# Layer 0's MLP in eight groups of 512 features, with seven block products from the third group on

## The chip, the cores and the metric

The kernel runs on one core of a Trainium2 chip. Its time is the time of one execution on the device in microseconds (us); three runs of the kernel before give 1492.6, 1496.15 and 1498.59 us, median 1496.15. One more execution was recorded by the profiler; all rows below are from that one.

A core has a matrix engine (PE; its weight loads are listed as PEld), a vector engine (DVE), a scalar engine (ACT), a general engine (POOL), and SP, which here only issues DMAs. Each works through its own instructions in a fixed order, and semaphores make one wait for another.

## The reference, cut to what matters

The program is a two-layer encoder trunk over 528 positions (512 frames and 16 meta tokens) of 1024 channels. Layer 0 has retention and an RG-LRU, layer 1 an S5 state space model and HGRN2; every layer ends with an MLP between two RMS norms:

```python
def rms_norm(x, g):
    return x * rsqrt(mean(x * x, axis=-1) + EPS) * g

# in each layer, D_FF = 4096
f = rms_norm(h, pre_g) @ w1            # 528x1024 @ 1024x4096
f = square(relu(f)) @ w2               # 528x4096 @ 4096x1024
h = h + rms_norm(f, post_g)
```

S5 needs factors that depend on its parameters only (powers of a complex number per state, their products with B and C, cosine and sine tables); layer 0's time is used to prepare them.

## The kernel before, in words

**Numbers.** All matrices are fp32. A factor is split into a rounded part (`wh`, `ah`, `nh`) and the rest (`wl`, `al`, `nl`), and a product is three matmuls: high by high, high by low, low by high (`three`, line 540). ACT writes the rounded part (CAST or ACTIVATE), DVE subtracts it to get the rest. Every weight matrix that is used thus costs ACT one cast and DVE (or POOL) one subtraction per element, besides its DMA.

**Layout.** Channels lie on the 128 partitions, positions along the free axis, in two halves of 264. A matmul takes 128x128 weights and 264 positions. `pair` gives a PSUM pair for both halves.

**Weights.** `weights` (line 410) writes down the order of all weight chunks of the program in a list, `plan`. `fetch` (439) issues a chunk's DMA to a `raw` buffer, `prepare` (460) splits all chunks up to a number, and `chunk` (474) hands out the next one after fetching two ahead and splitting one ahead. A chunk has 128x8x256 elements (1 MB).

**Order.** Each engine's order is that in which the Python program emits instructions. Work beside the matmuls is written as generators; `spawn` (373) puts one on a list, and `tick` (392), which the matrix loops call every few matmuls, lets those run whose time by a running estimate has come. A number that a generator yields is its wish for a pause. `drain` (403) runs all that is left.

**Layer 0's MLP** (`mlp0`, 1500) goes in four quarters of 1024 features. In a quarter, `mlp_in` (1374) multiplies by four chunks of the first matrix (tiles `m` on PE), and the result is squared after relu: ACT relu, ACT `ah`, ACT square into `mr`, DVE `mr`, DVE `al`. Then come four chunks of the second matrix, whose products DVE adds to eight accumulators `y` in SBUF. The last two chunks of the last quarter go through `gemm_trail` (722), which does all of the first half of the positions, then the second, so that the norm and the residual (`Stream.residual`, 897) of one half run beside the matmuls of the other. The next layer starts with `gemm_lead` (695), which takes the two halves likewise, with tiles `lead` on PE.

**Layer 1's MLP** does the first matrix of its last three quarters by seven block products instead of eight (Strassen's way in Winograd's form): channels and positions are each cut into halves, class `Seven` (630) makes sums and differences of weight blocks on POOL (`ws`, and in place in `raw`), splits them, and `seven_evac` (1452) joins the products `p` in PSUM into four results by seven additions on DVE (`mr`). The sums of the moving side are made once, before, by `moving_sums` (1407).

**S5's preparation** (`s5_prepare`, 1665) runs beside layer 0's MLP. `s5_common` (1558) makes the powers; `s5_half` (1611), eight times, the factors of four groups each: six POOL instructions of 128x512 in two runs of `powers` (`w`, `pt`, `m2`), transposes on PE, and small matmuls `k0`; `s5_tables` (1644), four times, the cosine and sine tables `ct`, `st` with scratch `tm`, by complex products (`cmul`, 362) on POOL. Tiles print as `m` for `m1`, `m2`, and `k` for `k0`.

Of the kernel before, what the change touches and what calls it, by code (L numbers as in the profile page):

```python
# [73 lines left out]
def trunk(ctx, tc, io, out, dbg=None):  # L74
# [436 lines left out]
    for l in range(2):  # L511
# [13 lines left out]
        for q in range(4):  # L525
            for i in range(4):
                seven = l == 1 and q > 0
                weights(w1s[l], 0, q * D + CW * i, order="S" if seven else "")
            if l == 0:
                for cc in range(4):  # L530
                    weights(w2s[l], q * D, CW * cc)
                continue
# [83 lines left out]

    def split_halves(i):
# [12 lines left out]
    class Seven:  # L630
# [7 lines left out]
        def __init__(self, n0, pairs):  # L638
            self.n0, self.pairs, self.n = n0, pairs, 14 * pairs
            self.fed, self.ops, self.s = 0, {}, {}  # L640

        def feed(self, upto):

            while self.fed < min(upto, self.n):
# [21 lines left out]
                (G if prod in ("P3", "P4") else V).tensor_tensor(lo, src, hi.bitcast(F32), SUB)  # L666
# [8 lines left out]
        def run(self, xops, evac):  # L675

            last = (self.n + 3) // 4 - 2
            for i in range(self.n):
                self.feed(i + 8 - i % 4 if i % 4 == 0 else i + 8)
# [7 lines left out]
                for k in range(4):  # L687
                    three(ps[:, e, :256], (hi, lo), k, 0, ops[k], k == 0, k == 3)
                    if k % 2:
                        tick()  # L690
                if e:
                    evac(pair_, prod, ps[:, :, :256])
# [173 lines left out]
    class Stream:  # L866
# [3 lines left out]
        def __init__(self, l, n, cut, keep=None, packed=True, lag=20.0):  # L870
            self.l, self.n, self.cut, self.keep, self.packed, self.lag = l, n, cut, keep, packed, lag
            self.ready, self.summed = [False, False], [False, False]
            self.sums = Squares(cut)
# [500 lines left out]
    def mlp_in(l, q, st):  # L1374
# [13 lines left out]

        if q == 0:
            gemm_lead([(w1s[l], 0, CW * i) for i in range(2)], st, cut, st.ready, evac)  # L1390
        elif l == 1:
            until(lambda: len(moving[4]) == 4)
            seven[0].run(lambda prod: moving_of(st, prod), seven_evac(a2))
            return a2
        for i in range(2 if q == 0 else 0, 4):
            wc = chunk(w1s[l], 0, q * D + CW * i)
# [8 lines left out]
    seven, moving = [None], {n: [] for n in (1, 2, 3, 4)}  # L1405

    def moving_sums(st):
# [3 lines left out]
        fst, snd = slice(0, 256), slice(256, 512)  # L1411
        for c in range(4):
            if c % 2 == 0:
                units = [(U("th", F32R), U("tl", F32R)) for _ in range(4)]
            cs = slice((c % 2) * 256, (c % 2) * 256 + 256)
# [17 lines left out]
            yield 3.0  # L1433

    def moving_of(st, prod):
        n = {"P5": 1, "P6": 2, "P7": 3, "P4": 4}.get(prod)
        if n:
            return moving[n]
# [3 lines left out]
    class Halves:  # L1442
# [5 lines left out]
        def __getitem__(self, at_):  # L1448
            c0, c1 = at_[1].start, at_[1].stop
            return self.parts[c0 // 256][:, c0 % 256 : c0 % 256 + c1 - c0]  # L1450

    def seven_evac(a2):
# [3 lines left out]
        def both(t):  # L1456
            return t[:, :512].rearrange("p (e w) -> p e w", e=2)

        def square(j, h, r):
            hi, lo = U("ah", F32R)[:, :512], U("al", F32R)[:, :512]  # L1460
# [6 lines left out]
        def evac(pair_, prod, ps):  # L1467
            def plus(dst, src):
                u.setdefault(dst, U("mr")[:, :512])
# [686 lines left out]
```

## Time and profile before

| what | value |
|---|---|
| profiled execution | 1494.63 us |
| its span | 1492.9 us |
| median of three runs | 1496.15 us |
| PE busy | 1438.3 us, 96% |
| DVE busy | 939.8 us, 63% |
| ACT busy | 613.8 us, 41% |
| POOL busy | 620.1 us, 42% |
| layer 0's MLP | from about 451 to 833 us |

The span runs from the first to the last recorded instruction; 1.73 us of the execution lie around it. Busy times are sums of durations as recorded: an instruction that is held up while it runs counts the holding as well. A group's line gives the mean of one instruction in nanoseconds, after the sum in microseconds.

### The profile page before, as it was taken

To read this page: it belongs to the slowest core of one execution; us is meant where nothing else is said; L and a number is where in the kernel's file an instruction comes from. 1 tells how busy PE (TensorE), PEld (TensorE's weight loads), DVE (VectorE), ACT (ScalarE), POOL (GpSimd) and SP (SyncE) were. 2 spreads that over 40 slices of the span, in tenths; PEclk is the share of its full clock that TensorE was granted. 3 is DMA by queue.
4 is the path that set the end of the run, shared out by engine and by line. 5 is a ranking of instruction groups with operands and counts; after the bars stand their busy time and mean duration, and the time that the engine had idled before them with its cause. 6 is when DMAs were issued, how large, how long until landed. Compare 5 with 4: busy or idle time off the path is not lost.

```text
span 1492.9 us, 26280 instructions
## 1 busy us (share of the span) xinstructions
PE 1438.3 (96%) x10744; PEld 1361.0 (91%) x10744; DVE 939.8 (63%) x1403; ACT 613.8 (41%) x1045; POOL 620.1 (42%) x703
## 2 busy tenths in 40 slices
PE   8999998999999999999999889998999999999997
PEld 6998898889999999999999889987898989898997
DVE  6787688765279636334344846839659867476565
ACT  6344373343137323233134432144445637345263
POOL 3535264333122995538511344445213235263434
PEclk9999999999999999999999999999999999999999
DMA  7315012303245343333343277531231415315141
GB/s 247 101 57 157 29 57 79 108 29 113 86 144 144 111 158 100 119 124 108 115 140 134 72 174 249 146 99 32 82 127 58 130 39 171 113 57 170 57 169 57
DMA packets 156968, 166.67 MB, mean 112 GB/s; under 512 B 30740, under 2 KB 127360, under 8 KB 156832
## 3 DMA queue, kind: packets, MB, share of 16 engines
q1 hardware_dynamic: 154320, 164.43, 35.0%
q8 instruction: 84, 1.38, 0.4%
q10 hardware_dynamic: 2176, 0.52, 0.2%
q14 instruction: 36, 0.29, 0.1%
q0 software_dynamic: 352, 0.05, 0.0%
HBM read 138.99 MB, written 22.74 MB: 108 GB/s over the span
## 4 chain that ended last, share of the span: by engine, by line
PE 77%; DVE 15%; ACT 2%; issue 2%; DMA 1%; POOL 1%; SPq 1%; DVEq 0%; ACTq 0%; POOLq 0%
PE m L140 35%; PE p L140 8%; PE wo L140 6%; PE v L140 4%; PE lead L140 3%; PE trail L140 3%; PE gt L140 2%; DVE wl L88 2%; PE av L140 2%; DVE m L88 2%; PE i L140 2%; DVE z L88 1%; PE hs L140 1%; PE ms L140 1%; DVE rt L88 1%
## 5 line engine op out<-in xcount | busy, mean ns | idle before, releaser
L88 DVE TENSOR_TENSOR wl<-raw,wh 128x1024 fp32r<-128x1024 f32 (+1 forms) x216 | 281.1, 1340 | 61.9 <-ACT wh L88 60.9
L88 ACT CAST wh<-raw 128x1024 fp32r<-128x1024 f32 (+1 forms) x252 | 223.3, 937 | 88.5 <-PE m L140 66.9
L140 PE MATMUL m<-nh,wh 128*128 128x264 f32 (+1 forms) x512 | 146.4, 286 | 0.0
L140 PE MATMUL m<-nl,wh 128*128 128x264 f32 (+1 forms) x512 | 145.5, 284 | 0.0
L140 PE MATMUL m<-nh,wl 128*128 128x264 f32 (+1 forms) x512 | 145.4, 284 | 0.0
L140 PE MATMUL m<-ah,wh 128*128 128x264 f32 x448 | 128.3, 286 | 0.0
L140 PE MATMUL m<-al,wh 128*128 128x264 f32 x448 | 127.3, 284 | 0.0
L140 PE MATMUL m<-ah,wl 128*128 128x264 f32 x448 | 127.3, 284 | 0.0
L88 POOL TENSOR_TENSOR sq<-sq,sq 128x264 f32<-128x264 f32 (+2 forms) x38 | 37.5, 989 | 176.7 <-ACT sq L88 174.0
L88 POOL TENSOR_TENSOR wl<-raw,wh 128x1024 fp32r<-128x1024 f32 (+1 forms) x36 | 74.7, 2092 | 76.5 <-ACT wh L88 76.4
L140 PE MATMUL m<-wh,ah 128*128 128x512 f32 (+1 forms) x288 | 106.2, 369 | 0.0
L140 PE MATMUL m<-wl,ah 128*128 128x512 f32 (+1 forms) x288 | 106.1, 368 | 0.0
L140 PE MATMUL m<-wh,al 128*128 128x512 f32 (+1 forms) x288 | 106.1, 368 | 0.0
L140 PEld LDWEIGHTS m<-nh,wh 128*128 128x128 f32 x512 | 96.3, 188 | 0.8 <-issue 0.7
L140 PEld LDWEIGHTS m<-nl,wh 128*128 128x128 f32 x512 | 96.5, 188 | 0.0
L140 PEld LDWEIGHTS m<-nh,wl 128*128 128x128 f32 x512 | 96.5, 188 | 0.0
L88 DVE TENSOR_TENSOR mr<-mr 128x528 f32<-128x528 f32 (+3 forms) x48 | 32.4, 677 | 90.8 <-ACT ah L88 89.5
L88 DVE TENSOR_TENSOR y<-m,y 128x528 f32<-128x528 f32 (+2 forms) x48 | 30.3, 649 | 87.5 <-PE m L140 87.5
L140 PEld LDWEIGHTS m<-ah,wh 128*128 128x128 f32 x448 | 84.3, 188 | 0.7 <-issue 0.7
L140 PE MATMUL lead<-nh,wh 128*128 128x264 f32 (+1 forms) x256 | 77.4, 302 | 7.2 <-ACT nh L88 6.6
L140 PEld LDWEIGHTS m<-al,wh 128*128 128x128 f32 x448 | 84.3, 188 | 0.0
L140 PEld LDWEIGHTS m<-ah,wl 128*128 128x128 f32 x448 | 84.2, 188 | 0.0
(473 smaller groups left out, 4836.1 us busy)
## 6 DMA issues: line engine op xcount, KB each, us to landing
raw<-mlp_w SPq DMA_DIRECT2D x52, 1024.0 KB, 5.5
raw<-w_in_ab SPq DMA_DIRECT2D x18, 1024.0 KB, 4.9
raw<-mlp_w SPq DMA_DIRECT2D x24, 512.0 KB, 4.6
raw<-w_in_cd SPq DMA_DIRECT2D x10, 1024.0 KB, 8.4
raw<-w_out_ab SPq DMA_DIRECT2D x8, 1024.0 KB, 5.0
hr<-hsp SPq DMA_DIRECT2D x16, 264.0 KB, 6.0
hsp<-h SPq DMA_DIRECT2D x8, 264.0 KB, 3.6
rbs<-rb SPq DMA_DIRECT2D x16, 132.0 KB, 2.2
```

Source lines behind the costliest of these rows:

```text
L88: i = f(*a, **k)
L140: return tc.keep_in_program_order(T.matmul(o, lhsT=l, rhs=r, start=a, stop=b))
```

## The change

- Layer 0's MLP goes in eight groups of 512 features: two chunks of the first matrix, then two of the second. The second matrix's chunks become 4x128 rows by 512 columns instead of 8x128 by 256; their size in bytes stays.
- From the third group on (`g > 1`: six groups) the first matrix goes by seven block products. A group then has 14 items (seven products, two 128-feature columns each) of 4 by 3 matmuls, 168, instead of 192. Of the low parts only those of product P4 are made by POOL there, the others by DVE.
- `moving_sums` is called for layer 0 too, and the long S5 work waits for it.
- S5's common factors are stored to a DRAM tensor `s5d` and loaded per eighth (`s5_keep`, `s5_load`); the work yields in smaller steps, and the complex products of the tables go from POOL to DVE.
- The trail has four parts of two 128-channel columns and four row blocks, instead of two parts of two columns and eight row blocks. Its second chunk is the one that is prepared ahead, and the chunk after it (the next layer's first) is prepared inside `gemm_trail`, in the second half of the positions.

```diff
@@ the list of weight chunks
+        for g in range(8 if l == 0 else 0):
+            for i in range(2):
+                weights(w1s[l], 0, 512 * g + CW * i, order="S" if g > 1 else "")
+            for e in range(2):
+                weights(w2s[l], 512 * g, 512 * e, 4)
...
@@ new: half 0 first, for the start of the second matrix
+    def gemm_late(pss, wc, xs, cut, ks):
+        for h in range(2):
+            for n, k in enumerate(ks[h]):
+                for j, ps in enumerate(pss):
+                    x = half_of(xs, k, cut, h)
+                    three(ps[:, h, : cut[h][1]], wc, k, j, x, n == 0, n == len(ks[h]) - 1)
+                tick()
@@ class Seven
-                (G if prod in ("P3", "P4") else V).tensor_tensor(lo, src, hi.bitcast(F32), SUB)
+                (G if prod in self.lows else V).tensor_tensor(lo, src, hi.bitcast(F32), SUB)
...
-                self.feed(i + 8 - i % 4 if i % 4 == 0 else i + 8)
+                self.feed(i + 8)
@@ gemm_trail
             for i, (j0, ops) in enumerate(parts):
+                if (h, i) == (1, 1):
+                    prepare(state["use"])
                 ps = pair("trail")
@@ mlp0
-        for q in range(4):
-            a2 = mlp_in(0, q, st)
...
+        for g in range(7):
+            a2 = mlp_in(0, g, st)
+            for e in range(2):
+                wc = chunk(w2s[0], 512 * g, 512 * e)
+                ahead = e and g
+                if ahead:
+                    seven[0] = Seven(state["use"], 1, 264, ("P4",))
+                    seven[0].feed(4)
+                for j in range(0, 4, 2):
                     pss = [pair("m2") for _ in range(2)]
...
+                        put(g, 4 * e + j + i, ps)
+                    if ahead and j == 0:
+                        seven[0].feed(8)
+        a2 = mlp_in(0, 7, st)
+        hs = reload(1, 0, 264)
         drain()
-        wcs = [chunk(w2s[0], 3 * D, CW * cc) for cc in (2, 3)]
-        parts = [(0, [(wc, k, a2) for k in range(KT)]) for wc in wcs]
+        wcs = [chunk(w2s[0], 7 * 512, 512 * e, 1 - e) for e in range(2)]
+        parts = [(j, [(wc, k, a2) for k in range(4)]) for wc in wcs for j in (0, 2)]
         gemm_trail(parts, ALL, evac, nxt.residual(y, sums, hs, 0, 3, ees[0]))
@@ S5: tables, and the frame of the preparation
-            cmul(G, cv[:, :, a : a + n], sv[:, :, a : a + n], cv[:, :, :n], sv[:, :, :n], er, ei, tv[:, :, :n])
-        yield 13.0
+            cmul(V, cv[:, :, a : a + n], sv[:, :, a : a + n], cv[:, :, :n], sv[:, :, :n], er, ei, tv[:, :, :n])
+            yield 1.0
...
+    s5d = dram("s5d", [8, P, 392])
+    def s5_load(q):
+        u = U("s5k")
+        dma(out=u[:, :392], in_=s5d[q])
+        return u
...
-    def s5_prepare():
+    def s5_prepare(st):
...
+        yield lambda: st.moving
+        load_s5()
+        yield 10.0
         yield from s5_common()
+        spawn(chain(s5_tables, range(4)))
+        u = s5_load(0)
+        yield 3.0
         for q in range(8):
-            yield from s5_half(q)
-            if q % 2:
-                yield from s5_tables(q // 2)
+            v = s5_load(q + 1) if q < 7 else None
+            yield from s5_half(q, u)
+            u = v
         s5_toeplitz()
-        pre.clear()
-
-    spawn(s5_prepare())
+    spawn(moving_sums(st))
+    spawn(s5_prepare(st))
```

The order in which the engines' instructions stand moves in two places that matter below. The first is DVE at the start of the trail of layer 0's MLP. Before, these rows lead into it (`y<-m` adds a second-matrix product, `y<-trail` one of the trail; `wl_8834` and `wl_8948` are the trail's chunks, `wl_8956` is layer 1's first chunk):

```order
L88 TENSOR_TENSOR wl_8834<-raw_8718,wh_8833 128x8x128 x2
L88 TENSOR_TENSOR y_4583<-m_1004_8839,y_4583 128x528
L88 TENSOR_TENSOR y_4584<-m_1006_8892,y_4584 128x528
L88 TENSOR_TENSOR wl_8948<-raw_8831,wh_8947 128x8x128 x2
L88 TENSOR_TENSOR wl_8956<-raw_8945,wh_8955 128x8x128 x2
L88 TENSOR_TENSOR y_4585<-trail_8969,y_4585 128x264
L88 TENSOR_TENSOR y_4586<-trail_8969,y_4586 128x264
```

Layer 1's first chunk thus stands ahead of all additions of the trail. At the end of the trail, on DVE too, these rows stand before (`nl` is the low part of layer 1's normed input, `sq` sums squares, `wl_9291` is layer 1's second chunk, `ve` begins the norm of the second half):

```order
L88 SCALAR_TENSOR_TENSOR nl_9155<-y_4586,vecs,nh_9154 128x264
L88 SCALAR_TENSOR_TENSOR nl_9161<-y_4587,vecs,nh_9160 128x264
L88 SCALAR_TENSOR_TENSOR nl_9165<-y_4588,vecs,nh_9164 128x264
L88 TENSOR_TENSOR sq_9190<-sq_9190,sq_9199 128x264
L88 TENSOR_TENSOR sq_9194<-sq_9194,sq_9205 128x264
L88 TENSOR_TENSOR wl_9291<-raw_8953,wh_9290 128x4x128 x4
L88 TENSOR_TENSOR ve_9332<-ms_9325,ee_5422 128x264
```

And now, at the same place (`wl_9515` is layer 1's first chunk, `wl_9645` its second):

```order
L88 SCALAR_TENSOR_TENSOR nl_9486<-y_4587,vecs,nh_9485 128x264
L88 SCALAR_TENSOR_TENSOR nl_9492<-y_4588,vecs,nh_9491 128x264
L88 SCALAR_TENSOR_TENSOR nl_9496<-y_4589,vecs,nh_9495 128x264
L88 TENSOR_TENSOR wl_9515<-raw_9265,wh_9514 128x8x128 x2
L88 TENSOR_TENSOR sq_9535<-sq_9535,sq_9544 128x264
L88 TENSOR_TENSOR sq_9539<-sq_9539,sq_9550 128x264
L88 TENSOR_TENSOR wl_9645<-raw_9273,wh_9644 128x4x128 x4
L88 TENSOR_TENSOR ve_9686<-ms_9679,ee_5436 128x264
```

Layer 1's first chunk has moved from before the trail's additions to behind them and behind the `nl`; its casts on ACT have moved with it, behind the eight `nh`. The second place is DVE in the middle of the MLP, while the tables are made. Before, the second quarter's rows read so:

```order
L88 TENSOR_TENSOR wl_6430<-raw_6187,wh_6429 128x8x128 x2
L88 TENSOR_TENSOR mr_6484<-mr_6484 128x528
L88 TENSOR_TENSOR al_6486<-mr_6484,ah_6485 128x528
L88 TENSOR_SCALAR st_6362<-st_6362,cols 128x528
L88 TENSOR_TENSOR mr_6540<-mr_6540 128x528
L88 TENSOR_TENSOR al_6542<-mr_6540,ah_6541 128x528
```

Now they read so in the fifth group's seven products:

```order
L88 TENSOR_TENSOR mr_7224<-p_932_7422,mr_7224 128x528
L88 TENSOR_TENSOR st_7132<-st_7132,tm_7133 128x8x2
L88 TENSOR_TENSOR tm_7342<-st_7341,epi_6655 128x8x2
L88 TENSOR_SCALAR st_7132<-st_7132,cols 128x528
L88 TENSOR_TENSOR ct_7340<-ct_7340,tm_7342 128x8x2
L88 TENSOR_TENSOR al_7417<-mr_7414,ah_7416 128x528
L88 TENSOR_TENSOR tm_7342<-st_7341,epr_6654 128x8x2
L88 TENSOR_TENSOR ct_7340<-ct_7340,epr_6690 128x8x4
L88 TENSOR_TENSOR st_7341<-ct_7340,epi_6691 128x8x4
L88 TENSOR_TENSOR mr_7224<-p_939_7471,mr_7224 128x528
```

Table rows now stand between those that empty PSUM (`mr<-p`) and make the second matrix's operands (`al`). In the stretch of 384 PE rows from the fourth group's second matrix to the fifth's, DVE has 113 of them, with 7376 elements per partition in all; in the next stretch, of 372 PE rows, 51 with 5072.

## Rows read from the trace of the kernel before

**Rows 1.** The page, busy time, share of the span, instructions of an engine
```profile
PE 1438.3 (96%) x10744; PEld 1361.0 (91%) x10744; DVE 939.8 (63%) x1403; ACT 613.8 (41%) x1045; POOL 620.1 (42%) x703
```

**Rows 2.** Windows: stretch, length, busy us of PE, PEld, DVE, ACT, POOL (count), clock, DMA
```profile
500.00:550.00 50.00, 50.00 (x419) 49.66 (x418) 17.41 (x18) 10.70 (x16) 48.39 (x115) 1.00 0.38 127
754.00:807.00 53.00, 53.00 (x436) 53.00 (x435) 20.76 (x25) 17.26 (x24) 2.66 (x2) 1.00 0.44 133
1315.00:1355.00 40.00, 40.00 (x339) 39.92 (x339) 32.32 (x36) 26.26 (x45) 24.50 (x16) 1.00 0.34 112
```

**Rows 3.** The chain of waits: start, us, what
```profile
753.72 52.98 PE m L140 x432
```

**Rows 4.** Groups of DVE instructions, 448 to 807 us: shapes, count, busy us, mean ns
```profile
L88 DVE TENSOR_TENSOR wl<-raw,wh 128x1024 fp32r<-128x1024 f32 x58 | 81.6, 1446 | 18.2 <-ACT wh L88 18.2
...
L88 DVE TENSOR_TENSOR y<-m,y 128x528 f32<-128x528 f32 x20 | 14.1, 705 | 49.8 <-PE m L140 49.8
...
L88 DVE SCALAR_TENSOR_TENSOR t<-ra,t 128x32 f32<-128x32 f32 x6 | 1.2, 192 | 0.2
```

**Rows 5.** Groups of DVE instructions in layer 1's seven products, 1315 to 1355 us
```profile
L88 DVE TENSOR_TENSOR mr<-p,mr 128x512 f32<-128x512 f32 x14 | 9.4, 683 | 3.6 <-PE p L140 3.4
L88 DVE TENSOR_TENSOR wl<-ws,wh 128x512 fp32r<-128x512 f32 x6 | 8.0, 1338 | 3.2 <-ACT wh L88 3.2
L88 DVE TENSOR_TENSOR wl<-raw,wh 128x512 fp32r<-128x512 f32 x6 | 7.8, 1312 | 0.0
L88 DVE TENSOR_TENSOR al<-mr,ah 128x512 fp32r<-128x512 f32 x6 | 5.3, 878 | 0.6 <-ACT mr L88 0.6
```

**Rows 6.** Groups of ACT instructions, same stretch
```profile
L88 ACT ACTIVATE mr<-mr 128x512 f32<-128x512 f32 x14 | 8.8, 632 | 10.2 <-DVE mr L88 10.0
```

**Rows 7.** Timeline of DVE in that stretch: start, us, instruction
```profile
1324.97 1.78 DVE L88 TENSOR_TENSOR wl<-ws,wh 128x512 fp32r<-128x512 f32 x1
...
1336.21 0.69 DVE L88 TENSOR_TENSOR wl<-raw,wh 128x512 fp32r<-128x512 f32 x1
1336.81 0.69 DVE L88 TENSOR_TENSOR wl<-ws,wh 128x512 fp32r<-128x512 f32 x1
```

**Rows 8.** POOL instructions by tile: ns least, median, most, where
```profile
L88 POOL TENSOR_TENSOR ws<-raw x12: 1282/1298/1767, 1214.1 to 1415.3; 128x512 f32<-128x512 f32 x12
...
L88 POOL TENSOR_TENSOR w<-b,pwb x8: 1056/1060/1974, 524.4 to 706.8; 128x512 f32<-128x512 f32 x8
L88 POOL TENSOR_TENSOR w<-w,pt x8: 1281/1294/2147, 527.6 to 708.9; 128x512 f32<-128x512 f32 x8
```

**Rows 9.** Timeline of DVE at the end of layer 0's MLP
```profile
812.03 3.88 DVE L88 TENSOR_TENSOR wl<-raw,wh 128x1024 fp32r<-128x1024 f32 x2 [0.15 <-ACT wh L88]
...
835.28 2.90 DVE L88 SCALAR_TENSOR_TENSOR nl<-y,vecs,nh 128x264 fp32r<-128x264 f32 x7
838.69 1.66 DVE L88 TENSOR_TENSOR sq<-sq,sq 128x264 f32<-128x264 f32 x2 [0.50 <-ACT sq L88]
841.51 4.00 DVE L88 TENSOR_TENSOR wl<-raw,wh 128x512 fp32r<-128x512 f32 x4 [1.16 <-ACT wh L88]
845.43 0.42 DVE L88 TENSOR_TENSOR ve<-ms,ee 128x264 f32<-128x264 f32 x1
```

**Rows 10.** Timeline of ACT, same place
```profile
808.08 5.84 ACT L88 CAST wh<-raw 128x1024 fp32r<-128x1024 f32 x4
...
833.42 3.35 ACT L88 ACTIVATE nh<-y,vecs 128x264 fp32r<-128x264 f32 x8 [8.95 <-DVE y L88]
836.68 3.85 ACT L88 ACTIVATE sq<-y 128x264 f32<-128x264 f32 x12
840.44 4.00 ACT L88 CAST wh<-raw 128x512 fp32r<-128x512 f32 x4
...
854.32 3.36 ACT L88 ACTIVATE nh<-y,vecs 128x264 fp32r<-128x264 f32 x8 [8.02 <-DVE y L88]
```

**Rows 11.** Waits of PE, 800 to 872 us: us in total, times, longest
```profile
PE lead L140 <- ACT nh L88: 4.2, 2, 2.5
```

More of the change, by code (lines that the diff above doesn't have):

```diff
@@ L524, in trunk @@
                     weights(wout1, r0, c0, 4, order=order)
-        for q in range(4):
-            for i in range(4):
[L527 to L532, printed above, removed]
+        for g in range(8 if l == 0 else 0):
[3 more added lines that the diff above has]
+                weights(w2s[l], 512 * g, 512 * e, 4)
+        for q in range(4 if l else 0):
+            for i in range(4):
+                weights(w1s[l], 0, q * D + CW * i, order="S" if q else "")
             for e in range(2):
@@ L872, in __init__ @@
             self.ready, self.summed = [False, False], [False, False]
-            self.sums = Squares(cut)
+            self.sums, self.moving = Squares(cut), None
             self.xs, self.hs, self.pk = [], [], {}
@@ L1387, in evac @@
                 relu2(ps[:, j, :w], rs[c][:, s], hi[:, s], lo[:, s], w)
+        n = 4 if l else 2
         if q == 0:
             gemm_lead([(w1s[l], 0, CW * i) for i in range(2)], st, cut, st.ready, evac)
-        elif l == 1:
-            until(lambda: len(moving[4]) == 4)
-            seven[0].run(lambda prod: moving_of(st, prod), seven_evac(a2))
-            return a2
-        for i in range(2 if q == 0 else 0, 4):
-            wc = chunk(w1s[l], 0, q * D + CW * i)
+        elif q > 1 - l:
+            until(lambda: st.moving)
+            seven[0].run(lambda prod: moving_of(st, prod), seven_evac(a2, w))
+            return a2
+        for i in range(2 if q == 0 else 0, n):
+            wc = chunk(w1s[l], 0, q * n * CW + CW * i)
             for j in range(2):
@@ L1403, in mlp_in @@
         return a2
-    seven, moving = [None], {n: [] for n in (1, 2, 3, 4)}
+    seven = [None]
     def moving_sums(st):
@@ L1410, in moving_sums @@
         yield 3.0
-        fst, snd = slice(0, 256), slice(256, 512)
+        w = st.cut[0][1]
+        fst, snd = slice(0, w), slice(w, 2 * w)
+        moving = {n: [] for n in (1, 2, 3, 4)}
         for c in range(4):
@@ L1433, in moving_sums @@
             yield 3.0
+        st.moving = moving
     def moving_of(st, prod):
@@ L1503, in evac @@
         def evac(h, i, j, ap):
[L1504 removed]
+            c = 2 * i + j
             s = slice(264 * h, 264 * h + 264)
             V.tensor_tensor(y[c][:, s], ap, y[c][:, s], ADD)
[L1507 to L1530 removed]
+            sums.add(y[c][:, s], (h,), f"G{c}" if c > 3 else "G")
@@ L1578, in s5_common @@
                 G.tensor_copy(vb[i][:, :, t], vf[i][:, :, 7 - t])
+            yield 2.0
+        for i in range(2):
+            s5_keep(pf[i], 256 + 36 * i, 36)
+            s5_keep(pb[i], 328 + 32 * i, 32)
+        yield 2.0
         b2, bs = s5raw[:2]
@@ L1663, in s5_tables, with chain @@
         dma(out=sind[:, q], in_=st)
-    def s5_prepare():
+    def chain(f, ids):
+        for i in ids:
+            yield from f(i)
+    def s5_prepare(st):
         yield 10.0
@@ L1787, in s5_quad @@
         gx[q] = split(g5, SEQ, "g5")
-    def chain(f, ids):
-        for i in ids:
-            yield from f(i)
     us = [U("up") for _ in range(4)]
@@ L2109, in trunk @@
                 if ahead:
-                    seven[0] = Seven(state["use"], 2)
+                    seven[0] = Seven(state["use"], 2, 256, ("P3", "P4"))
                     seven[0].feed(4)
```

117 lines of the change are left out of this document (61 added, 56 removed).

## The prediction

> **What bounds the kernel now.** I read the busy shares of the page first: PE is at work in 96% of the span [rows 1], so only two things move the time by much: fewer matmuls, or idle time of PE that is added or taken away. The windows say where such idle time is. In layer 0's MLP there is none: in 500 to 550 and in 754 to 807 us PE is busy throughout, at the full clock of 2.4 GHz, though POOL is busy for 48.39 of 50 us in the first of them [rows 2]. The chain of waits agrees: between 753.72 and 806.70 us it is 432 matmuls and nothing else, 52.98 / 432 = 0.1226 us each [rows 3]. A matmul taken out of this stretch is worth 0.1226 us as long as everything that feeds PE keeps up. The same kind of work as the new one is already there in layer 1: in 1315 to 1355 us the seven products run with PE busy for 40.00 of 40 us, DVE for 32.32 and POOL for 24.50 [rows 2]. Only behind the trail does PE wait, for the normed input of the next layer, 4.2 us in two waits [rows 11].
>
> **The removed work.** Six groups, each 168 matmuls for 192: 6 x 24 = 144 matmuls of 264 columns, 144 x 0.1226 = 17.7 us. Additions in PSUM are not paid for on PE. What is added goes to DVE and POOL, and to the places where the stages meet.
>
> **DVE in a group.** One group, from one second matrix to the next, is 168 + 192 = 360 matmuls, 44.1 us. DVE's own part in it, in durations that nothing holds up: 12 low parts of 512 at 0.69 (the undisturbed ones [rows 7]) 8.3, 4 of 1024 at 1.446 [rows 4] 5.8, 7 `mr` at 0.70 (0.683 at 512 elements [rows 5]) and 4 `al`, taken like them, 7.7, 8 `y` at 0.705 [rows 4] 5.6; 27.4 us together. Three rows show two more things. Successive instructions start 0.60 us apart though each lasts 0.69 [rows 7], so 0.09 us of each is beside its neighbour. And the same low part that takes 0.69 takes 1.78 us while POOL computes [rows 7]. In the layer 1 stretch 12 low parts average 1.33 instead of 0.69 and 6 `al` 0.878 instead of 0.70 [rows 5], 8.8 us in all over 16 POOL instructions [rows 2], or 0.55 us of DVE per POOL instruction.
>
> **The tables.** A 32-element DVE instruction takes 0.192 and a 528-element one 0.705 us [rows 4], thus 0.159 us and 1.03 ns per element. All four tables are some 170 such instructions, and most fall in two stretches. In that of 384 PE rows (47.1 us) there are 113 with 7376 elements: 18.0 + 7.6 = 25.6 us, and 1.4 for two scalings. With DVE's own 27.4 that is 54.4 in durations; less 0.09 for each of some 148 instructions, 41.1 us. POOL has 15 instructions of 512 there; at 0.55 they make 8.3, and DVE comes to 49.4 of 47.1, 2.3 too much. In the next stretch of 372 PE rows (45.6 us), 51 instructions with 5072 elements are 13.3 us; 27.4 + 13.3 + 1.4 - 7.9 + 21 x 0.55 = 45.8 of 45.6, 0.2 too much. In the first stretch 25 table rows stand between a `y` addition and the first emptying of a product; at 0.1 to 0.25 us each that is 3 to 6 us, and a PSUM pair is needed again 48 matmuls (5.9 us) after it is full. I add 1.5 us for such bunches and take 4 us for the tables. The ends are 0, when DVE's idle time takes it all (41.1 is below 47.1), and 24, worked out as the last rival.
>
> **POOL** loses the tables and gets eight sums and two low parts per group, 10 x 1.28 = 12.8 us, beside the S5 eighths of 4 x 1.06 + 2 x 1.28 = 6.8 us [rows 8]. Even two eighths and the sums are 26.4 of 44.1 us; POOL by itself is not late.
>
> **Where the first matrix meets the second.** After the last product a result goes through a DVE addition (0.70), three ACT steps (3 x 0.632 [rows 6]) and `al` (0.70): some 3.3 us with DVE and ACT free. PE needs it 32 to 46 rows on, 3.9 to 5.6 us. Only the fifth group has table rows inside this path (some 1 to 2.5 us); I take 0.7 us for all six, between 0 and 6 (1 us each). The last two eighths of S5 are 13.6 us on POOL beside the last group's 168 matmuls, 20.6 us, and PE needs their end before the trail: 0.5 us, between 0 and 4. The moving sums (on DVE 28 instructions of 264 elements, between 0.192 and 0.705 us each [rows 4]) lie in the first two groups, which use none of them yet; 0.
>
> **The seam to layer 1.** Here something moves onto the path. Layer 1's first chunk was cast by ACT (5.84 us for four casts, 1.46 each [rows 10]) and split by DVE (3.88 us for two [rows 9]) at 808 to 816 us, beside the trail's matmuls, at no cost. Now both stand behind the `nh` and `nl` of the first half. On ACT `nh` ends at 836.8; two squares and the first cast take it to 838.9, the second to 840.4, and the remaining squares and layer 1's second chunk come 2.9 us later than before (840.44 [rows 10]). On DVE `nl` ends at 838.2 [rows 9]; the two splits run from about 838.9 to 842.8. PE's lead, which began with the first `nh`, can't pass its sixth matmul until the second split is done. That is not yet the price, since lead's first half had slack: what decides is `ve`, the start of the second half's norm. It stands behind the four small splits of the second chunk, which began at 841.51 and ended at 845.5 [rows 9]. Now `sq` (1.66) follows at 842.8 and those splits at 844.5, so `ve` goes from 845.43 to about 848.5: 3.0 us. Also `ve` needs a sum that PE makes 24 matmuls into lead, at 846 to 848.5 by full or half clock. The second half's `nh` (854.32 [rows 10]) and the second half of lead follow. I take 4.0 us, between 0 (`ve` was late for another reason) and 8 (the whole shift of lead's first half is kept).
>
> **The sum.** -17.7 + 4.0 (tables) + 1.2 (transitions and end of S5) + 4.0 (seam) = -8.5 us. The profiled execution of 1494.63 us (span 1492.9 and 1.73 around it) becomes 1486.1; the median of the runs shown lies 1.5 us above that execution, so I say 1487.7 against 1496.15 us. Within 0.5%, 7.5 us, a measurement of this kernel does not tell a difference from none; the forecast lies just beyond, below 1488.7.
>
> **Rivals.**
>
> A. The matmuls' worth in full but for the seam. DVE's idle time takes up the tables and the transitions hold; the seam costs 3: 1496.15 - 17.7 + 3.0 = 1481.5 us. For it: 41.1 us of DVE in 47.1, and the layer 1 stretch, where PE never waits at DVE 32.32 of 40 [rows 2]. Against it: no stretch of that kind has table rows in it.
>
> B. The tables take what the matmuls give. Overlap between successive instructions is lost where one reads what the last wrote, as in a complex product, and half of the last rival's excess is met: 12 us; 1496.15 - 17.7 + 12 + 1.2 + 4 = 1495.7 us, no change.
>
> C. Slower: DVE and POOL can't work side by side. The 1.78 us for 0.69 [rows 7] is then a POOL instruction waited out, and the two engines' instructions of two SBUF operands add up. In the first table stretch DVE has 8.3 + 5.8 + 2.8 + 25.6 = 42.5 us of them and POOL 9 x 1.28 + 6.8 = 18.3: 60.8 of 47.1 us, 13.7 too many. In the second 8.3 + 5.8 + 2.8 + 13.3 = 30.2 and 10 x 1.28 + 11 x 1.13 = 25.2: 55.4 of 45.6, 9.8 too many. 23.5 us of stalls make 1496.15 - 17.7 + 23.5 + 5.2 = 1507 us. It decides from the point where the sum of the two is above PE's time; from 13 us of stalls on there is no gain. For it: the long low parts [rows 7] come in just the length of a POOL instruction, and the eight `w` go up to 1.97 us [rows 8]. Against it: 0.55 us per POOL instruction in the layer 1 stretch, where half the instructions ran undisturbed, and much of a table is small instructions whose 0.159 us need not all hold a port.
>
> The Trainium skill, SBUF — State Buffer, section "Who interferes with whom", states this rule: a DVE instruction with two SBUF inputs and a GpSimd instruction that reads SBUF take turns at one shared pair of ports, each for its whole length. By that rule rival C would hold in full and the time would be 1507 us; the trace agrees as far as single instructions go (1.78 for 0.69 us), and on the sum of a stretch no row here decides, since the layer 1 stretch adds up to less than its 40 us.
>
> That the change doesn't do what it says I leave out: the order has 144 PE rows less and the table rows on DVE.
>
> **How the numbers follow.** The forecast's case (stalls of 2 to 8 us, 1484 to 1492 us) gets 0.40, and about two thirds of it lie below 1488.7; A gets 0.25, B 0.20 (1492 to 1502), C 0.15. Faster: 0.27 + 0.25 = 0.52; within 0.5%: 0.13 + 0.19 = 0.32; slower, above 1503.6: 0.16. The likeliest case's own range is 1484 to 1492. The range for 8 in 10 goes from 1479 (A without any cost at the seam is 1478.5) to 1504, up to rival C.
>
> **What would show it.** The seven products' PE stretches should be 20.6 us in each of six groups, and PE without waits in 590 to 640 and from 730 us. Waits of PE for DVE `mr`, `wl` or `y` should add up to 2 to 6 us between 630 and 730 us, and DVE's busy time in that stretch should be near its length. Low parts of 512 should average 1.0 to 1.4 us while POOL is at work. Lead should begin 6 to 8 us later after the trail's end than before, with ACT casting behind `nh`, and `ve` 3 to 5 us later. Waits above 20 us in the middle would make C right; none there, A. The forecast is wrong at its root if PE waits in every group, also in those without tables, or if the last group waits for POOL before the trail.

## The result and the profile after

The changed kernel is slower: 1517.91 us (median of four runs, 1515.08 to 1518.41) against 1494.83 us (1492.6 to 1498.59), a ratio of 1.0148 [1.0122, 1.0174]. The forecast was 1487.7 us, and 1517.9 lies above its whole range. The profiled execution has a span of 1516.3 us, 23.4 more than before.

The first part of the page, to be read beside [rows 1]:

```profile
PE 1432.6 (94%) x10600; PEld 1351.7 (89%) x10600; DVE 1066.6 (70%) x1701; ACT 663.6 (44%) x1159; POOL 643.6 (42%) x602
```

The 144 matmuls are gone. PE's busy time fell by only 5.7 us, and the span grew: both idle time and slower matmuls were added.

Three marks in the timelines of PE place them: M, the first matmul of `m` in layer 0's MLP; T, the first of `trail`; F, the first of `f` in layer 1. M to T is called the MLP stretch below, T to F the seam.

```
               M        T        F       span    M to T   T to F
before       463.15   806.54   871.76   1492.9    343.4    65.2
after        463.46   827.0    898.61   1516.3    363.5    71.6
```

So 20.1 us arise in the MLP stretch and 6.4 in the seam. The rest, -3.1, is the start (0.3) and what follows F, which ranges from 615.5 to 622.2 us over the profiles of this study, without a cause that I can name. Windows of the kernel after, with the columns of [rows 2]:

```profile
505.00:600.00 95.00, 89.20 (x718) 88.81 (x717) 63.35 (x86) 37.62 (x64) 65.14 (x127) 0.96 0.43 114
600.00:712.00 112.00, 97.76 (x754) 94.96 (x753) 104.19 (x239) 39.71 (x63) 52.33 (x46) 0.95 0.34 115
712.00:830.00 118.00, 113.22 (x938) 110.15 (x937) 84.59 (x87) 57.31 (x91) 78.23 (x51) 0.97 0.38 125
```

Before, stretches here had PE busy from end to end at a clock of 1.00 [rows 2]; the middle window then read:

```profile
600.00:712.00 112.00, 112.00 (x945) 110.64 (x944) 46.09 (x46) 33.85 (x44) 66.20 (x107) 1.00 0.35 110
```

Now every window has idle time of PE and a clock below 1. In the middle one DVE is busy for 104.19 of 112 us, and PE gets 754 matmuls through where 112 / 0.1226 = 913 would fit. What PE waited for, 505 to 850 us (total, times, longest):

```profile
PE p L140 <- DVE y L88: 6.4, 2, 5.6
PE m L140 <- DVE y L88: 4.9, 5, 2.6
PE m L144 <- ACT m L88: 4.3, 1, 4.3
PE p L140 <- DVE mr L88: 3.0, 1, 3.0
PE p L140 <- DVE wl L88: 2.8, 1, 2.8
PE m L140 <- DVE al L88: 1.9, 3, 1.1
PE m L140 <- DVE st L88: 1.2, 1, 1.2
```

With the last row of the answer, 0.3 us, these are 24.8 us. Nearly all of it lies in three places: 5.6 us at 581 us, ahead of the second of the six groups of seven products (in the first row); some 14 us between 600 and 712 us, for DVE; and 4.3 us at 820 us, for the end of S5 (the third). The stretch's balance is -17.7 (matmuls) + 24.8 (waits) + 13.0 (the remainder) = +20.1. Most of the remainder is the clock. Its deficit in the three windows is 95 x 0.04 + 112 x 0.05 + 118 x 0.03 = 12.9 us, but a part of that lies inside waits. The trace has four periods of the lower level, 1.2 GHz, in the stretch, from 583.6, 621.2, 706.5 and 822.6 us on, 24.9 us in all. PE is idle for 6.2 us of them and works for 18.7, which at half of 2.4 GHz costs 9.4 us. The other 3.6 us stay without a cause, and no run took the clock away by itself.

**The first wait.** POOL made the sums for the first group of seven products from 510 to 538 us. This is its timeline ahead of the second group's (start, us, instruction, count):

```profile
561.19 1.28 POOL L88 TENSOR_TENSOR t<-pwf,ar 128x32 f32<-128x32 f32 x1
562.44 1.25 POOL L88 TENSOR_TENSOR pwf<-pwf,ar 128x32 f32<-128x32 f32 x1
563.64 0.27 POOL L88 TENSOR_TENSOR pwf<-pwf,ai 128x32 f32<-128x32 f32 x1
...
566.55 2.24 POOL L88 COPY pwb<-pwf 128x32 f32<-128x32 f32 x9
...
571.18 1.28 POOL L88 TENSOR_TENSOR ws<-raw 128x512 f32<-128x512 f32 x1
```

From 539.3 to 571.1 us POOL is busy for 31.53 of 31.80 us with 99 instructions, nearly all of them S5's small ones; the second group's first sum `ws` stands behind them. DVE then:

```profile
574.63 2.67 DVE L88 TENSOR_TENSOR wl<-ws,wh 128x512 fp32r<-128x512 f32 x1 [4.06 <-ACT wh L88]
577.22 0.69 DVE L88 TENSOR_TENSOR y<-m,y 128x528 f32<-128x528 f32 x1
579.35 4.38 DVE L88 TENSOR_TENSOR wl<-ws,wh 128x512 fp32r<-128x512 f32 x1 [1.43 <-ACT wh L88]
```

The low parts of the sums come late, and take 2.67 and 4.38 us instead of 0.69 [rows 7] because POOL is adding the next ones. The `y` additions behind them free PE's PSUM pair, and PE resumes like this:

```profile
580.87 0.28 PE L140 MATMUL m<-ah,wl 128*128 128x264 f32 x1
586.76 0.56 PE L140 MATMUL p<-nh,wh 128*128 128x264 f32 x1 [5.61 <-DVE y L88]
587.11 0.42 PE L140 MATMUL p<-nl,wh 128*128 128x264 f32 x1
```

Successive matmuls now start 0.22 us apart, not 0.12, until 590.4 us. The windows around show the granted clock:

```profile
570.00:580.00 10.00, 9.81 (x81) 9.60 (x80) 4.51 (x4) 1.82 (x4) 10.00 (x15) 1.00 0.37 55
580.00:588.00 8.00, 2.40 (x16) 2.21 (x15) 7.84 (x6) 1.19 (x2) 7.29 (x6) 0.73 0.02 1
588.00:592.00 4.00, 4.00 (x25) 4.00 (x25) 0.00 (x0) 0.40 (x1) 3.75 (x4) 0.69 0.04 6
592.00:600.00 8.00, 8.00 (x68) 8.00 (x67) 4.53 (x7) 4.73 (x9) 1.76 (x2) 1.00 0.89 296
```

Between 588 and 592 us PE works without a gap and does 25 matmuls where 33 fit at full clock: the mean of 0.69 lies between the two levels of 1.2 and 2.4 GHz. The lower one lasted from 583.6 to 590.5 us: it began inside the wait, and PE worked under it for 3.7 us.

**The middle.** DVE and POOL side by side around 616 us, DVE first:

```profile
616.41 0.16 DVE L88 TENSOR_TENSOR tm<-st,s 128x8 f32<-128x8 f32 x1
616.49 1.27 DVE L88 TENSOR_TENSOR st<-ct,s 128x8 f32<-128x8 f32 x1
...
618.80 1.23 DVE L88 TENSOR_TENSOR ct<-ct,tm 128x8 f32<-128x8 f32 x1
...
627.15 1.25 DVE L88 TENSOR_TENSOR st<-st,tm 128x16 f32<-128x16 f32 x1
```

```profile
616.42 1.30 POOL L88 TENSOR_TENSOR ws<-raw 128x512 f32<-128x512 f32 x1
617.80 2.21 POOL L88 TENSOR_TENSOR ws<-ws,raw 128x512 f32<-128x512 f32 x1
619.97 2.33 POOL L88 TENSOR_TENSOR raw<-raw 128x512 f32<-128x512 f32 x1
```

A table row of 8 elements takes 0.16 us, or 1.27 us when a POOL instruction runs: the row of 616.49 us ends at 617.76, POOL's instruction at 617.72. POOL suffers too: 1.28 us [rows 8] become 2.21 and 2.33. Not every row is held: 5 of the 24 rows of 8 elements and 19 of all 168 table rows took more than 1 us.

**The seam.** ACT behind the trail, then PE:

```profile
855.16 3.35 ACT L88 ACTIVATE nh<-y,vecs 128x264 fp32r<-128x264 f32 x8 [8.98 <-DVE y L88]
858.42 0.72 ACT L88 ACTIVATE sq<-y 128x264 f32<-128x264 f32 x2
859.05 3.75 ACT L88 CAST wh<-raw 128x1024 fp32r<-128x1024 f32 x2
862.71 4.49 ACT L88 ACTIVATE sq<-y 128x264 f32<-128x264 f32 x14
867.11 4.00 ACT L88 CAST wh<-raw 128x512 fp32r<-128x512 f32 x4
```

```profile
861.01 0.59 PE L140 MATMUL lead<-nh,wh 128*128 128x264 f32 x1 [6.96 <-ACT wh L88]
```

This is the order of [rows 10] with the casts moved as predicted, but the two take 3.75 us, not 2.9. The prediction's 1.46 us was a mean over the four casts of [rows 10]: the two of the trail's chunk took 1.04 us each, and the two of layer 1's first chunk 2.03. They have not become longer; they were long before. `ve` starts at 872.18, 45.18 after T; before it was 845.43 [rows 9], 38.89 after T.

### The profile page after: what moved, and what is told of

The parts are those of the page before. It is cut to its first block, busy times and chain, and to the rows that moved or that the text cites. A ratio compares the mean times of both kernels' runs of the same rounds, so it can differ in the third digit from the quotient of the medians.

```text
span 1516.3 us, 26456 instructions
## 1 busy us (share of the span) xinstructions
PE 1432.6 (94%) x10600; PEld 1351.7 (89%) x10600; DVE 1066.6 (70%) x1701; ACT 663.6 (44%) x1159; POOL 643.6 (42%) x602
## 4 chain that ended last, share of the span: by engine, by line
PE 62%; DVE 22%; ACT 5%; POOL 4%; issue 4%; DMA 2%; SPq 1%; DVEq 0%; ACTq 0%; POOLq 0%
PE m L140 18%; PE p L140 10%; PE wo L140 6%; DVE wl L88 5%; PE v L140 4%; PE trail L140 3%; PE lead L140 2%; PE gt L140 2%; ACT wh L88 2%; PE av L140 2%; DVE m L88 2%; DVE y L88 2%; PE i L140 2%; SPq L147 1%; PE hs L140 1%
## 5 line engine op out<-in xcount | busy, mean ns | idle before, releaser
L88 ACT CAST wh<-raw 128x1024 fp32r<-128x1024 f32 (+1 forms) x276 | 228.2, 872 | 141.8 <-PE m L140 64.3
L88 POOL TENSOR_TENSOR wl<-raw,wh 128x512 fp32r<-128x512 f32 (+1 forms) x48 | 91.2, 1913 | 87.0 <-ACT wh L88 86.8
L140 PE MATMUL p<-th,wh 128*128 128x264 f32 (+1 forms) x384 | 110.7, 288 | 4.1 <-DVE mr L88 3.0
L140 PE MATMUL p<-th,wl 128*128 128x264 f32 (+1 forms) x384 | 109.7, 286 | 2.8 <-DVE wl L88 2.8
L140 PE MATMUL p<-tl,wh 128*128 128x264 f32 (+1 forms) x384 | 109.6, 286 | 0.0
L88 DVE TENSOR_TENSOR wl<-ws,wh 128x512 fp32r<-128x512 f32 x60 | 70.0, 1185 | 42.4 <-ACT wh L88 42.4
L88 ACT ACTIVATE mr<-mr 128x528 f32<-128x528 f32 (+1 forms) x96 | 60.6, 638 | 75.0 <-DVE mr L88 73.4
L88 POOL TENSOR_TENSOR ws<-raw 128x512 f32<-128x512 f32 x24 | 35.2, 1465 | 135.8 <-DMA raw<-mlp_w 106.1
L140 PE MATMUL p<-nh,wh 128*128 128x264 f32 (+1 forms) x288 | 83.1, 289 | 5.6 <-DVE y L88 5.6
L88 DVE TENSOR_TENSOR y<-m,y 128x528 f32<-128x528 f32 (+2 forms) x76 | 49.2, 666 | 47.7 <-PE m L140 47.5
```

The source lines that it names most:

```text
L88: i = f(*a, **k)
L140: return tc.keep_in_program_order(T.matmul(o, lhsT=l, rhs=r, start=a, stop=b))
```

## The experiments

The theory: three costs, the tables (DVE against POOL in the middle), POOL's queue at the second group's sums (which the expectations call the first), and the seam. The rivals: DVE is simply overloaded; the seven products don't work in this stretch at all; POOL's own time is the limit. The ratios are to the kernel before, timed on the same chip. Edits are cut to what matters.

**The tables left out.** (`e_notab`)
```
-  cmul(V, cv[a:a+n], sv[a:a+n], ...)
+  G.memset(cv[:, :, a : a + n], 1.0)
+  G.memset(sv[:, :, a : a + n], 0.0)
```


> The changed kernel without the complex products of S5's tables: memsets on POOL stand in their place, so the tables hold no cosines. Theory (DVE and POOL take turns at SBUF, and each short table instruction on DVE waits out a POOL instruction): the waits of PE between 600 and 712 us, 14 us in the trace of the changed kernel, and the matmuls at the lower clock behind them go, about 20 us, so 1498 us; the first wait near 587 us, the one before the trail and the lead's stay. Rival (POOL's sums come late on their own, for the S5 work ahead of them in POOL's queue): under 6 us, so 1512 us or more.

1502.16 us, 1.0052 [1.0034, 1.0071], between the two expectations and nearer to the theory's. The MLP stretch falls from 363.5 to 344.7, the waits of 600 to 712 us nearly vanish, and the window has its matmuls again:

```profile
600.00:712.00 112.00, 109.74 (x915) 108.10 (x914) 82.22 (x90) 53.85 (x84) 70.50 (x110) 1.00 0.48 157
```

The tables cost 15.7 us, not 4. The lower clock is a part of this: in the stretch it lasts for 10.0 us here, 24.9 in after. The tables don't explain the rest: 5.6, 4.3 and 7.0 us of waits stand in the trace as before.

**The tables on POOL.** (`e_tabpool`)
```
-  cmul(V, ...)
+  cmul(G, ...)
```


> The changed kernel with the tables' complex products back on POOL. Theory (the engines take turns): little is won, 1508 to 1518 us, since the same instructions of two SBUF operands now stand in POOL's queue ahead of the sums, and DVE's low parts wait for them. Rival (DVE simply has more to do than fits): all of the table stretch comes back, 1498 us, with DVE's waits gone.

1535.64 us, 1.0276 [1.0251, 1.0301]: worse than either theory said. With sums in its queue POOL can't carry the tables: PE waits 6.5 us for POOL's `wl`, 5.5 for ACT's `wh` and 5.1 for DVE's `mr`. Moving the tables to DVE was right by 17.7 us; the sums had taken away the place they came from.

**S5's factors left out.** (`e_nos5`)
```
-  load_s5() ... s5_common(), s5_tables, s5_half x8, s5_toeplitz()
+  zeros to m1d, m2d, m3d, cosd, sind
```


> The changed kernel without S5's preparation beside the MLP, except its parameters: zeros are stored in place of the factors. Theory (all waits in the MLP come from S5's work on POOL and DVE): PE runs through from the second group to the trail, and the full worth of 144 matmuls, 17.7 us, less the seam of 4 to 6 us, is there: 1481 to 1483 us. Rival (the seven products feed PE too late by themselves, by their sums and low parts): waits stay in every group, 1490 us or more.

1478.36 us, 0.9885 [0.987, 0.99], M to T 320.25 us, a little below the expected 1481 to 1483. The seven products themselves run; what they lack in after is the room that S5 takes. PE's own work for S5 (some 12 to 13 us of matmuls) is gone here too, so this is no estimate of what a better order could give.

**The seam undone.** (`e_seam`)
```
-  if (h, i) == (1, 1): prepare(state["use"])
-  wcs = [chunk(w2s[0], 7 * 512, 512 * e, 1 - e) ...]
+  wcs = [chunk(w2s[0], 7 * 512, 512 * e) ...]
```


> The changed kernel with layer 1's first chunk split ahead of the trail, as before the change. The prediction put 4.0 us on this, and the trace of the changed kernel has a wait of 7.0 us of the lead for the cast. Theory (the price is what the second half's norm is late by): 4 to 6 us less, 1512 to 1514 us. Rival (lead waits as long for the normed input): under 2 us, 1516 us or more.

1529.3 us, 1.0227 [1.0205, 1.0248]: a miss of 15 us. T to F grows from 71.6 to 76.3, which is 4.7 of the 11.4 us over after; the MLP stretch stays (363.2), and the rest is not explained. SP's timeline, then ACT's:

```profile
831.12 6.86 SPq L147 DMA_DIRECT2D m3d<-k0d  x8
838.08 1.22 SPq L147 DMA_DIRECT2D raw<-w_in_cd  x2
```

```profile
843.59 3.77 ACT L88 CAST wh<-raw 128x1024 fp32r<-128x1024 f32 x2 [12.18 <-DMA raw<-w_in_cd]
```

Layer 1's first weights are issued on SP behind the eight transfers that end S5. S5 ends later than before (there the eight began at 769 us), so ACT, whose cast now comes first, stood for 12.18 us with the squares queued behind it, and PE waited 6.8 us for `sq`. The seam and S5's end belong together.

**Both: S5 left out and the seam undone.** (the two edits above)

> Without S5's preparation, as in the run e_nos5 (1478.4 us), and with layer 1's first chunk split ahead of the trail. Theory (splitting it ahead failed in the run e_seam only because the chunk's DMA stood on SP behind the end of S5's work, so that ACT's cast waited for it): with that work gone the seam is as before the change, from the trail's start to layer 1's next matrix 65 us instead of 71, and the time is 4 to 6 us less, 1472 to 1474 us. Rival (the trail of four parts is what costs): no change, 1477 to 1480 us.

1471.49 us, 0.9838 [0.9824, 0.9853], just below the expected 1472 to 1474. The seam is 67.2 us (65 were expected, as before the change) against 70.5 with S5 out alone: the moved casts cost some 3 us where SP's queue is free. The times differ by 6.9 us, of which the few microseconds that vary behind F are a part.

**S5 begun earlier.** (`e_early`)
```
+  yield 4.0 and s5_common() ahead of   yield lambda: st.moving
```


> The changed kernel with S5's common factors (about 110 short POOL instructions) no longer waiting for the moving sums: they stand in POOL's queue before the first sums of weight blocks instead of before them in time only by their own pace. Theory (the first wait of PE, 5.6 us near 587 us, comes from POOL: its queue holds the short S5 instructions from 539 to 571 us ahead of the sums): this wait and the slow matmuls behind it go, 6 to 8 us, 1510 to 1512 us. Rival (DVE's low parts and additions are late there by themselves): under 2 us, 1516 us or more.

1512.05 us, 1.0109 [1.0094, 1.0124], at the upper end of the expected 1510 to 1512. The wait at 581 us is gone, while 600 to 712 us stays much as it was (769 matmuls, clock 0.95). So the first wait comes from POOL's queue and not from the tables. Its price alone the run does not give: S5 also ends earlier, and the wait of 4.3 us at 820 is gone with it. The MLP stretch is 9.7 us shorter, the two waits were 9.9.

**Plain groups in the new arrangement.** (`e_plain`)
```
-  weights(w1s[l], 0, ..., order="S" if g > 1 else "")
+  weights(w1s[l], 0, ..., order="")
-  elif q > 1 - l:          ahead = e and g
+  elif l and q:            ahead = False
```


> The changed kernel with eight block products, as before, in all groups: groups of 512, the new order of S5's preparation, tables on DVE and the new trail stay. Theory (S5's rearranged work does no harm where the groups need no sums and fewer low parts): from the start of the MLP to its trail 343 to 347 us, as before the change, plus the seam and the end of S5: 1500 to 1508 us. Rival (the rearrangement itself costs): the waits of the table stretch are there too, 1515 us or more.

1506.91 us, 1.0075 [1.0062, 1.0088]. Without one seven-product group the new arrangement costs 10.8 us against the 1496.11 of the kernel before on that chip; in the profiles, 7.5 in the stretch, which at 350.9 us is above the expected 343 to 347, and 6.5 in the seam. Of the 7.5 us, 4.7 are waits. In this order the products add 11.0 us to it (1506.91 to 1517.91), though they take 17.7 us of matmuls away.

**POOL's reads taken away, in two steps.** First the product that makes S5's powers (`e_nopow`), then also the four sums (`e_noreads`):
```
-  G.tensor_tensor(a, b..., pw_..., MUL); G.tensor_tensor(dst, dst, t1, ADD)
+  G.memset(a, 0.0); G.memset(dst[:, :512], 0.0)
```


> The changed kernel with memsets, which read nothing, in place of the 48 POOL instructions that make S5's eighths; the factors are thus zeros, and the tables stay on DVE. Theory (turns at SBUF between DVE and POOL instructions that read two operands): in the stretch of the tables a third to a half of the waits goes, as the sums of weight blocks remain, and the wait before the trail (4.3 us and the slow matmuls behind it) too: 10 to 16 us less, 1502 to 1508 us. Rival (DVE's own instructions are too many there, whatever POOL does): only the wait before the trail goes, 5 to 7 us, 1511 to 1513 us.

```
-  G.tensor_tensor(s[e, 1], a[1, 0], a[1, 1], ADD)   (and three more)
+  G.memset(s[e, 1], 0.25)
```


> As the run e_nopow, with memsets also in place of the sums of weight blocks on POOL (in both layers; the sums are constants, not sums): of POOL's long instructions only the low parts of one product still read SBUF, and all the table rows stay on DVE. Theory (turns at SBUF between the two engines): the waits of PE between 600 and 712 us, 14.0 us in the change and 5.9 in e_nopow, fall below 3 us, and the MLP's part up to the trail from 348 to 341 to 345 us: 1496 to 1500 us. Rival (what is left in e_nopow is DVE's own load): 5 us or more of waits stay there, 1500 to 1503 us.

1502.5 us, 1.0046 [1.0033, 1.0058], the lower end of what the theory said, and 1488.67 us, 0.9958 [0.9943, 0.9973], 7 us below it. The tables stay on DVE in both. First the windows, the one kernel and then the other:

```profile
600.00:712.00 112.00, 106.35 (x866) 103.36 (x865) 103.71 (x253) 46.54 (x74) 42.36 (x46) 0.98 0.45 147
```

```profile
600.00:712.00 112.00, 111.48 (x932) 110.08 (x931) 96.52 (x260) 51.69 (x83) 26.43 (x52) 1.00 0.46 156
```

With DVE busy for 96.52 of 112 us, more instructions than in after, PE is idle for 0.52 us. A DVE that is merely overloaded is thus excluded: with 86% of the stretch busy it serves PE. Its low parts say what changed, after and then the kernel without reads (count, busy us, mean ns):

```profile
L88 DVE TENSOR_TENSOR wl<-raw,wh 128x512 fp32r<-128x512 f32 x12 | 11.4, 962 | 2.2 <-ACT wh L88 2.2
...
L88 DVE TENSOR_TENSOR wl<-ws,wh 128x512 fp32r<-128x512 f32 x10 | 9.1, 918 | 0.0
```

```profile
L88 DVE TENSOR_TENSOR wl<-raw,wh 128x512 fp32r<-128x512 f32 x15 | 10.1, 687 | 1.7 <-ACT wh L88 1.7
L88 DVE TENSOR_TENSOR wl<-ws,wh 128x512 fp32r<-128x512 f32 x12 | 8.1, 685 | 0.3 <-ACT wh L88 0.2
```

They are back at 0.69 us, and the 24 table rows of 8 elements take 0.17 us on average instead of 0.40. One confound stays: a memset is shorter (0.53 us against 1.28), so POOL's queue empties sooner as well. That is in part how the second run beat its expectation: the wait at 581 us, 6.1 us in the first, is 1.9 in it. But where after lost its time DVE's low parts of sums had no idle time ahead of them (0.0 above): DVE was not waiting for POOL's results, its own instructions were long.

**The seven products later.** Five kernels have S5 begun early, its tables ahead of its common factors, and the old seam, and use the products from various groups on (counted from 0, as in the code; in after they begin with group 2). First from group 4 on (`f3_seven_late`, whose edit is shown), and from group 2 on (`f1_seven_early`):
```
-  order="S" if g > 1        elif q > 1 - l
+  order="S" if g > 3        elif q > (0 if l else 3)
-  yield 10.0 if q == 0 else 6.0      (s5_half; also 5.0, 3.0)
+  yield 10.0 if q == 0 else 2.0      (also 2.0, 1.5)
```


> Seven products from the fifth group on (four groups, 96 matmuls less, 11.8 us); S5's preparation starts earlier, the tables first, and goes in shorter pauses, so that the tables end before the first group of seven products and the eighths some 900 matmuls before the trail; layer 1's first chunk is split ahead of the trail. Theory (the seven products pay when S5's work is out of their way and its end out of the trail's): 1494.8 - 11.8 and 2 to 5 us of waits, 1485 to 1488 us. Rival (the two engines are too full in any order): 1495 us or more.

> As the run f3_seven_late but with seven products from the third group on, as in the change: S5's tables and half of its eighths stand among the first groups of seven products. Theory (turns at SBUF): the waits of the table stretch stay, some 15 to 20 us, but the seam and the end of S5 (6 + 7 us) and part of the first wait are won: 1500 to 1506 us, slower than f3_seven_late in spite of 48 matmuls less. Rival (only the order of POOL's queue and the end of S5 mattered): 1482 us or less.

1496.49 us, 1.0001 [0.9992, 1.0011], and 1525.85 us, 1.0197 [1.018, 1.0214]: both miss upwards, the first into its rival's range. In it PE has one long wait in the stretch, in S5's transposes:

```profile
688.11 1.12 PE L144 MATMUL m<-ident,w 128*128 128x128 f32 x4 [5.56 <-POOL w L88]
```

S5's eighths were now so close that PE reached a transpose before POOL, with sums ahead of the power product in its queue. The second is slower than after itself, by 11.1 us in the MLP stretch (374.7 us): its waits there add up to 29.8 us (after: 24.8), and 44.4 us of it lie at the lower clock (24.9). No run takes its causes apart. Then with the eighths apart again and S5's start closer, from group 4 (`f10_late_loose`), 5 (`f11_later_loose`) and 3 (`f12_third`):
```
-  yield 2.0 / 2.0 / 1.5     (s5_common)
+  yield 0.8 / 0.8 / 0.8
-  yield 10.0 if q == 0 else 2.0;  2.0;  1.5     (s5_half)
+  yield 10.0 if q == 0 else 5.0;  1.5;  1.0
```


> As the run f3_seven_late (four groups with seven products, tables first, no waits but 7 us from S5's eighths and 2 in the first new group), with the eighths spread: more room between an eighth's POOL instructions and the PE transposes that need them. Theory (the 5.6 us wait there is PE standing in its own queue for a late POOL): 5 to 7 us less than f3_seven_late's 1496.5, so 1489 to 1492 us. Rival (POOL is late by as much at any such place): 1495 us or more.

> As f10_late_loose with seven products from the sixth group on (three groups, 72 matmuls less, 8.8 us). Theory: fewer of S5's eighths lie beside the seven products, and what is left of waits is 1 to 3 us; 1488 to 1492 us, about f10_late_loose's time. Rival (waits are due to S5's work itself): 1494 us or more.

> As f10_late_loose with seven products from the fourth group on (five groups, 120 matmuls less): the last of S5's tables and all of its eighths now lie beside them. Theory (tables and eighths beside the sums cost more than 24 matmuls, 2.9 us, per group): slower than f10_late_loose's 1489.7, 1494 to 1502 us. Rival (one more group pays as the others): 1486 to 1488 us.

```
seven products from group   4          5          3
time, us                 1489.73    1490.53    1497.21
ratio                     0.9961     0.9969     1.0007
95%                    0.9949-0.9973 0.9959-0.998 0.9997-1.0017
M to T, us                339.3      340.45     348.1
```

From group 4 on the time is 0.9961 of before's, with an interval below 1, and all three times are within what was expected. With group 4 the tables lie between 524 and 611 us, in plain groups and ahead of the first sum on POOL (612 us), and the window that was the worst reads:

```profile
600.00:712.00 112.00, 108.94 (x921) 106.86 (x921) 83.87 (x92) 47.64 (x78) 77.25 (x53) 1.00 0.38 124
```

Four seven-product groups are worth 96 x 0.1226 = 11.8 us of matmuls; the gain is 0.39%, 5.8 us, and 4.1 us of the stretch, in which the clock never falls. One group earlier takes it all back: there the tables (until 630 us) meet the sums (from 562 us), and PE waits 5.9 us for table rows. S5's first eighths lie there too, and no run parts the two.

## Why the prediction was wrong

**The removed work** held: 144 matmuls fewer at 0.1226 us.

**The tables** are the first failed step: 4 us said, 15.7 measured. What failed is the way from DVE's load to PE's wait, the overlap. The rows' own time held: 38.9 us for 164 of them in the sum, 42.3 for all 168 in the run without POOL's reads. The price of a meeting, 0.55 us per POOL instruction [rows 5], nearly held: from 600 to 712 us DVE's instructions took some 32 us more than the shortest of their tile and shape, 0.69 for each of POOL's 46 (an estimate, counted from the traces). But I set sums against idle time. The two table stretches were 95.2 us of DVE for 756 PE rows (49.4 + 45.8), 2.5 more than PE's time, so little seemed to be lost. The window has 104.19 us of DVE for 754 matmuls, and 7.8 us in which DVE is idle all the same: idle time at one moment doesn't serve another, when PE's next PSUM pair hangs on a DVE instruction behind a held one. The window is 19.6 us longer than its matmuls need (112 - 754 x 0.1226), waits and clock together.

That is close to rival C, with a chance of 0.15: it had DVE's and POOL's two-operand instructions add up, to 116.2 us for the two stretches (60.8 + 55.4), and put 23.5 us on them. The Trainium skill, SBUF — State Buffer, section "Who interferes with whom", says that the two engines take turns at one pair of ports; the trace agrees (1.27 for 0.16 us, and 0.685 us low parts once the reads are gone). In whole runs 15.7 us hung on the tables, and 29.2 us on POOL's long instructions (1517.91 to 1488.67), the first wait included. The two numbers overlap: tables or powers taken away give 15.7 and 15.4 us, though not all the same waits.

**"POOL by itself is not late"** is the second. 26.4 of 44.1 us was a sum over a group; what counted was the queue at one moment, and the sum left out S5's common factors. 99 instructions in 31.8 us, nearly all theirs, stood ahead of the second group's sums. The run that began S5 earlier was 5.9 us faster, which includes the end of S5.

**The moving sums at 0**, done in the groups before they are used: their own cost was not isolated.

**The clock** was not in the sum at all. I priced a wait at its length. Behind the 5.6 us wait PE worked for 3.7 us at the lower level, and in the whole stretch for 18.7 us, which cost 9.4.

**The end of S5**, 0.5 us said within 0 to 4, was a wait of 4.3, and not through POOL, whose last instruction for it ended at 819.5 us. PE waited for ACT's copy of an earlier transpose, which stood in ACT's queue behind the steps of the last products:

```profile
822.90 0.64 ACT L88 ACTIVATE mr<-mr 128x528 f32<-128x528 f32 x1
823.45 0.57 ACT L88 COPY m<-m 128x512 f32<-128x512 f32 x1
```

**The seam**, 4.0 said, was 6.4, inside its range of 0 to 8. Its path was as said (`nh`, casts, splits, `ve`); `ve` came 6.3 us later after T instead of 3.0. The two moved casts, priced by a mean over unlike ones, are 0.8 us of the difference; 1.3 us were there already when `nh` began (28.2 us after T, 26.9 before).

**In sum**, the prediction had costs of 5.2 us in the MLP stretch against the 17.7 of removed work. They were 37.8: 24.8 of waits, 9.4 of the clock, 3.6 without a cause. By the runs, 18.9 us of the stretch go with the tables and 9.7 with an earlier S5; the other 9 us no run assigns.

**Of what would show it**: PE without waits failed at 610 and 619 us (1.1 and 2.6 us) and at 820; waits of 2 to 6 us between 630 and 730 were some 10; the products' six stretches, 20.6 us said, took 20.9 to 28.5; DVE's busy time near the stretch's length and lead 6 to 8 us later held (96.22 of 100 us; 6.6 after T). Waits not above 20 us in the middle (14) spoke against C as priced, though its mechanism was at work: C's stalls are waits and clock together, 19.6 us. The range ended at 1504, short of C's 1507, and C was given neither POOL's queue nor a larger price for the end of S5 on top: costs of separate mechanisms add up, and a range over single rivals does not hold their sum.

## What to carry to other kernels

Fewer matmuls are worth their time only where the engines that prepare them have room at that moment: put a new preparing step where no other two-operand work runs on DVE and POOL at once, and start it after the old bunch is done. An engine whose sum of work just fills a stretch is late by more than the excess: here 2.5 us too much by the sum went with a cost of 15.7, and behind waits PE worked at the lower clock. A mean is only as good as what it averages: four casts of 1.46 us were two of 1.04 and two of 2.03. And look at what stands ahead of a new instruction in each queue, SP's and ACT's too, since moving the end of a stage moves what was issued behind it.

## What was not expected of the hardware

- A DVE instruction of 8 elements took 1.27 us instead of 0.16 beside a POOL instruction of 1.30, and POOL's own went from 1.28 to 2.33 us.
- In a wait of PE of 5.61 us the granted clock fell, and behind it matmuls started 0.22 us apart for 3.7 us. After the 2.96 us wait that ended at 656.9 us they started 0.12 us apart from the second on.
- ACT's casts of 128x1024 weights took 1.04 us, but the two of layer 1's first chunk, the only ones whose source is read in another order (8 x 16 x 8 elements instead of rows of 128 or 256), took 1.91 to 2.08 in every profile of this study, before the change as well as after. No run changes the order alone.
